# A branch between two expert groups, a deferred embedding, and a last tile in two halves

## The chip, the cores and the metric

The kernel runs on one core of a Trainium2 chip. The metric is the device time of one execution in microseconds (us); lower is better. The core has a matrix engine (PE, with PEld for its weight loads), a vector engine (DVE), a scalar engine (ACT), GpSimd (POOL), and SP, which here only issues transfers. All transfers, from whichever queue, run on the same 16 DMA engines.

## What is computed

One layer: a state-space branch and a convolution branch, an output projection, a layer norm, a mixture of experts, a second layer norm, a gated embedding, and a third layer norm. Only the last three stages bear on the change:

```python
m = hierarchical_moe(h, ...)        # 512 tokens; each goes to 2 of 32 experts
# gate, up = t @ w_gate[e], t @ w_up[e]     (2048 -> 256 each)
# out      = (silu(gate) * up * weight) @ w_down[e]
h = layer_norm(ALPHA * h + m, ln2_g, ln2_b)
e = (p @ w_p) * sigmoid(h @ w_pg + b_pg)    # 2048 -> 2048
x = layer_norm(ALPHA * h + e, ln3_g, ln3_b)
```

Each expert has 6 MB of float32 weights, 192 MB in all, and each is read once.

## The kernel before, in words

**Expert stage.** The 32 experts stand in 14 groups (`GROUPS`), of one, two or four experts each. A group takes up to 128 token rows. The first two groups have two fixed experts each; which experts the others serve is read at run time. A group goes through these steps:

- `gather(i)` (line 1109): POOL fetches the group's token rows into `gx` by an indirect transfer.
- `columns()` (line 1118): PE transposes `gx` in four steps of four blocks; DVE and ACT copy the results to `xt`. There is one `gx` and one `xt`.
- `up` (line 1139), four stages q: each needs one 1 MB load of `w_gu` per expert.
- `act` (line 1146): sigmoid, products, two transposes.
- `down` (line 1159), two stages, each with one 1 MB load of `w_dn` per expert; the result goes to `ob`, and POOL scatters it to `y_dram`.

All weight loads are issued by SP in one order into a ring of 1 MB tiles (`ring_load`, line 1103). A tile is loaded again when PE has read it. The ring has 15 tiles. During group 0 they take that group's 12 loads and the first three of group 1. At the end of group 1 (line 1213) two tiles from the pool `rpool` are put at the front of the ring, so that the next two loads go there. Until then these two tiles hold `w_p`, which the deferred piece of the embedding (lines 1206 to 1212) reads: for the last of the four token tiles, `p @ w_p` is computed after group 1, in 8 products of 512 columns, and written to `p_dram` in two transfers.

**The branch.** If a fixed group has more tokens than its strips hold, an overflow block runs (line 1226). The count is put in `mo` (line 1224), which is the first column of `xt`, so it is written after group 0's first stage has read that column. Every engine reads it into a register and branches by itself. Inputs here take the way around the block. At the end of the way around, SP waits until all the transfers it has issued have landed. The block uses `gx`, `xt` and `ob`. For this reason group 1's gather and columns stand behind it (lines 1279 and 1280), while from group 1 on, the next group's gather stands ahead of `up` and its columns ahead of `down` (lines 1195 and 1200):

```python
if i + 1 < NGR and i:
    gather(sl0[:, i + 1:i + 2])
```

**Order of the work.** The order within each engine's queue is set by a planner with its own model of times; it may move an instruction ahead of the branch if the block doesn't touch what it needs. The program's order gives the priorities.

**Final stage.** For each of four column blocks c of 512 and each token tile m, `f_mm` (line 1330) makes 48 products of 512 columns (16 blocks of the depth, three products each, float32r operands: high and low parts). `gate` (line 1338) adds the bias (DVE), takes the sigmoid (ACT), multiplies by the embedding, adds to `h2` and takes `bn_stats`, all on 512 columns. In the last block, the third layer norm follows for each tile: statistics, a chain of small DVE steps for the inverse root (`rsqrt`), and two passes over two pieces of 1024 columns (`layer_norm`, line 178), each piece then written out (line 1437).

Of the kernel before, what the change touches and what calls it, by code (L numbers as in the profile page):

```python
# [54 lines left out]
def build(tc, I, out, dbg=None, stages=9):  # L55
# [1022 lines left out]
    if True:  # L1078
# [30 lines left out]
        def gather(ig):  # L1109
            G.indirect_dma_start(out=gx, out_offset=None, in_=h_dram,  # L1110
                                 in_offset=bass.IndirectOffsetOnAxis(ap=ig, axis=0), bounds_check=S - 1, oob_is_err=False)
# [75 lines left out]
        early = [loads(0, q) for q in range(6)]  # L1187
        ahead1 = [loads(1, 0)]
        gather(sl1)
        V.tensor_copy(ids_, tab[:, 0:NP])  # L1190
        columns()
        for i, (width, members) in enumerate(GROUPS):
            st = strips(width, members)
            gu = bank("gu", 2)
            if i + 1 < NGR and i:
                gather(sl0[:, i + 1:i + 2])
            for q in range(4):
                up(gu, st, early[q] if i == 0 else ahead1[q] if i == 1 and q < 2 else loads(i, q), q)
            at = act(gu, wt0[:, i:i + 1])
            if i + 1 < NGR and i:  # L1200
                columns()
            for q in range(2):
                down(at, st, early[4 + q] if i == 0 else loads(i, 4 + q), q, sl0[:, NGR + i:NGR + i + 1])
            if i == 1:

                for q in range(2):
                    for c in range(2):
                        ps = bank("dps", 4)
                        for k in range(2):
                            T.matmul(ps, pm[:, k], wps[q][:, k, c * 512:(c + 1) * 512], start=k == 0, stop=k == 1)  # L1210
                        (A.copy if c else V.tensor_copy)(pe_[:, c], ps)
                    G.dma_start(p_dram[NT - 1, 2 * q:2 * q + 2].rearrange("c p d -> p c d"), pe_)
                ring[:0] = [rpool.tile([P, D], FT, name="raw", tag="raw", bufs=2) for _ in range(2)]
            if i == 2:
                for m in range(NT):
                    A.activation(tt[m], tt[m], AF.Identity, scale=ALPHA, bias=zero_of(at[:, 0, 0:1]))
            if i:
                continue
            ahead1.append(loads(1, 1))
            nc.sync.dma_start(pm, I["pT"][:, :, (NT - 1) * P:])  # L1220


            mo = xt[:, 0, 0:1].bitcast(I32)
            V.tensor_copy(mo, tab[:, 2 * NP:])
            most = nc.values_load(mo[0:1], min_val=0, max_val=S)
            with tc.If(most > 0):
                cv, cg = Carve(ob), Carve(gx)
                sv, place = cv.tile([P, 3, 2 * NT]), cv.tile([P, NP])
                pb, v4 = [P, 2 * NT, NP], [P, 2 * NT, 2, NP]
                nc.sync.dma_start(sv.rearrange("p a n -> p (a n)"), sv_dram)  # L1230
                nc.sync.dma_start(place, I["place"][0:1].broadcast_to([P, NP]))
                iot, iof, z = cv.tile([P, P], I32), cv.tile([P, P]), cv.tile([P, 2 * NP])
                tokv, slx = cv.tile([P, 2, NT, 2]), cv.tile([P, NOV, 3 * NP], I32)
                hot = cg.tile([P, 2 * NT, P])
                by_place, vw, val = cv.tile(pb), cv.tile(pb), cg.tile(v4)
                G.iota(iot, pattern=[[1, P]], base=0, channel_multiplier=0)
                V.tensor_copy(iof, iot)
                iop = iot[:, 0:NT]
                G.iota(iop, pattern=[[P, NT]], base=1, channel_multiplier=1)
                for j in range(2):  # L1240
                    V.tensor_copy(tokv[:, j, :, 0], iop)
                    V.tensor_scalar(tokv[:, j, :, 1], tokv[:, j, :, 0], 2.0, float(j - 1), op0=OP.mult, op1=OP.add)
                V.tensor_tensor(by_place, place.unsqueeze(1).broadcast_to(pb), sv[:, 1].unsqueeze(2).broadcast_to(pb), op=OP.is_equal)
                V.tensor_tensor(val, by_place.unsqueeze(2).broadcast_to(v4),
                                tokv.rearrange("p j t a -> p (j t) a").unsqueeze(3).broadcast_to(v4), op=OP.mult)
                V.tensor_tensor(vw, by_place, sv[:, 2].unsqueeze(2).broadcast_to(pb), op=OP.mult)
                for c in range(NOV):
                    slot_hot(hot, iof, sv[:, 0])
                    slot_rows(slx[:, c, 0:2 * NP], hot, z, val.rearrange("p n a e -> p n (a e)"), bank("gu", 2), 2 * NP)
                    slot_weights(slx[:, c, 2 * NP:].bitcast(FT), hot, vw, bank("gu", 2), NP)  # L1250
                    V.tensor_scalar(sv[:, 0], sv[:, 0], -float(P), None, op0=OP.add)
                nc.sync.dma_start(ov_dram, slx)
                V.memset(gx, 0.0)

                with tc.For_i(0, NP, 1) as n:
                    mine = nc.values_load(tab[0:1, bass.ds(n + NP, 1)], min_val=0, max_val=S)
                    with tc.If(mine > 0):
                        e = bass.ds(nc.values_load(tab[0:1, bass.ds(n, 1)], min_val=0, max_val=NE - 1), 1)
                        for c in range(NOV):
                            with tc.If(mine > c * P):  # L1260
                                so = ep.tile([P, 3], I32, name="so")
                                for a in range(3):
                                    nc.sync.dma_start(so[:, a:a + 1], ov_dram[:, c, bass.ds(n + a * NP, 1)])
                                gather(so[:, 0:1])
                                columns()

                                def chunk(q):
                                    nc.sync.dma_start(gx, part(e, q))
                                    return [gx]

                                whole = [(0, slice(0, P))]
                                gu = bank("gu", 2)
                                for q in range(4):
                                    up(gu, whole, chunk(q), q)
                                at = act(gu, so[:, 2:3].bitcast(FT))
                                for q in range(2):
                                    down(at, whole, chunk(4 + q), q, so[:, 1:2])
                                V.memset(gx, 0.0)
            gather(sl0[:, 1:2])
            columns()  # L1280

    s5.close()

# [1 line left out]
    with ExitStack() as s5:  # L1285
# [8 lines left out]
        fpws = [fh.tile([P, 512], FT, name=f"fpw{j}") for j in range(2)]  # L1294
        fsgs = [fh.tile([P, 512], FT, name=f"fsg{j}") for j in range(2)]
        bpgs = [fh.tile([P, 512], FT, name=f"bpg{j}") for j in range(2)]
        st3 = fh.tile([P, NT, 4, 6], FT, name="st3")
        wF = s5.enter_context(tc.tile_pool(reuse_waits="tile", name="wF", bufs=1))
        fystk = ExitStack()
        fy = fystk.enter_context(tc.tile_pool(reuse_waits="tile", name="fy", bufs=1))  # L1300
# [26 lines left out]
        hls.append(wsplit(wF, raws[3], 8, (G, G)))  # L1327
        w_pg = ahead([lambda c=c, q=q: wsplit(wF, raw_load(I["w_pg"][c, q]), 8) for c in range(1, 4) for q in range(4)], 1)

        def f_mm(ps, m, q, hl):  # L1330
            ms = slice(m * P, (m + 1) * P)
            for kk in range(4):
                wh, wl = hl[kk // 2]
                wv = slice(kk % 2 * 512, kk % 2 * 512 + 512)
                k = 4 * q + kk
                mm3(ps, h2h[:, k, ms], h2l[:, k, ms], wh[:, wv], wl[:, wv], k == 0, k == KD - 1)

        def gate(m, c, ps, bpg):
            cs_ = slice(c * 512, (c + 1) * 512)
            flip[0] ^= 1  # L1340
            o, sg = fpws[flip[0]], fsgs[flip[0]]
            nc.sync.dma_start(o, p_dram[m, c])
            V.tensor_tensor(sg, ps, bpg, op=OP.add)
            A.activation(sg, sg, AF.Sigmoid)
            V.tensor_tensor(sg, o, sg, op=OP.mult)
            V.scalar_tensor_tensor(h2[m][:, cs_], h2[m][:, cs_], ALPHA, sg, op0=OP.mult, op1=OP.add)
            V.bn_stats(st3[:, m, c], h2[m][:, cs_])

        def after(x, v):

# [46 lines left out]
        for c in range(4):  # L1397
# [18 lines left out]
            for m in range(NT):  # L1416
                if c == 0:
# [3 lines left out]
                    if m == NT - 1:  # L1421
# [1 line left out]
                        for t in (bpgs[0], bpgs[1], *fpws):  # L1423
                            V.tensor_copy(t[:, 0:1], h2l[:, KD - 1, S - 1:S].bitcast(FT))
                        A.dma_start(bpg, I["b_pg"][:, 0:512].broadcast_to([P, 512]))
                for q in range(4):
                    f_mm(ps[m], m, q, hls[q])
                if c == 0 and m == NT - 1:
                    for j in range(NT):
                        gate(j, c, ps[j], bpg)  # L1430
                if c == 3:
                    gate(m, c, ps[m], bpg)
                    mean, rstd = ln_stats(fh, st3[:, m], "s")
                    for q in range(2):
                        i = slice(q * 1024, (q + 1) * 1024)
                        layer_norm(h2[m][:, i], h2[m][:, i], mean, rstd, g3[:, i], b3[:, i])
                        nc.sync.dma_start(out[m * P:(m + 1) * P, i], h2[m][:, i])
    top.close()
# [64 lines left out]
```

## Time and profile before

| what | us |
|---|---|
| median of 3 runs (1487.8 to 1489.32) | 1488.04 |
| the profiled execution | 1486.21 |
| its span in the trace | 1484.5 |
| PE busy | 1264.4 (85%) |
| DVE busy | 784.1 (53%) |
| POOL busy | 392.9 (26%) |
| ACT busy | 376.4 (25%) |

The profiled execution took 1.71 us more than its span; that part lies around the trace. Busy shares are means over stages with different limits, so they are read by stretch. In the trace, the expert stage reaches from about 667 to 1236 us and the final stage from there to 1484.5 us.

### The profile page before, as it was taken

The numbers are of one execution on the slowest core, as the hardware profiler recorded it, in microseconds if no ns is written. First come the engines' busy times: TensorE is split into PE (matmuls) and PEld (weight loads), VectorE is DVE, ScalarE is ACT, GpSimd is POOL, SyncE is SP. The second block draws the span as 40 slices with busy tenths as digits, with TensorE's granted clock in tenths as the row PEclk, the third lists the DMA queues.
The fourth block names the chain that finished last, engine by engine and source line by source line (L and its number), as shares of the span: only waits on it lengthen the run. The fifth ranks groups of instructions, "written<-read, shape, count | busy, mean of one in ns | idle before, by whom it ended". The sixth has DMA issues, their size and how long they took to land.

```text
span 1484.5 us, 16536 instructions
## 1 busy us (share of the span) xinstructions
PE 1264.4 (85%) x6128; PEld 805.0 (54%) x6129; DVE 784.1 (53%) x1275; ACT 376.4 (25%) x568; POOL 392.9 (26%) x327
## 2 busy tenths in 40 slices
PE   6999999989999999978488998787767774599996
PEld 4877878777777888843132322221111121388884
DVE  7999899789997643681011110010000006975567
ACT  4336555554333421121012100000000003023210
POOL 0368667864944200010010110000000005600000
PEclk9999999998999999989699999999889996699998
DMA  6344544536531362349659999999999995426413
GB/s 233 110 132 119 153 145 137 146 115 217 218 120 59 115 223 85 110 175 375 271 220 424 422 422 421 420 419 420 418 409 418 415 386 190 142 105 215 141 44 120
DMA packets 97448, 349.90 MB, mean 236 GB/s; under 512 B 29939, under 2 KB 43779, under 8 KB 61707
## 3 DMA queue, kind: packets, MB, share of 16 engines
q1 hardware_dynamic: 51152, 303.21, 52.4%
q10 hardware_dynamic: 38832, 21.38, 5.3%
q0 software_dynamic: 7376, 24.19, 4.2%
q8 instruction: 50, 0.82, 0.2%
q14 instruction: 38, 0.30, 0.1%
HBM read 324.36 MB, written 36.38 MB: 243 GB/s over the span
## 4 chain that ended last, share of the span: by engine, by line
DMA 27%; PE 19%; DVE 4%; issue 1%; ACT 0%; POOL 0%; SPq 0%; DVEq 0%; POOLq 0%; ACTq 0%
DMA ring<-w_gu 16%; DMA ring<-w_dn 8%; PE gu L1144 4%; PE fps L102 3%; PE fps L101 3%; PE fps L100 3%; PE dps L1165 2%; DMA raw<-w_gu 2%; DVE tt L180 1%; PE xtp L1124 1%; DMA gx<-h_dram,sl 1%; DVE tt L181 1%; PE h2p L102 0%; PE h2p L101 0%; PE h2p L100 0%
## 5 line engine op out<-in xcount | busy, mean ns | idle before, releaser
L1144 PE MATMUL gu<-ring,xt 128*32 128x512 f32 (+2 forms) x1112 | 241.3, 654 | 57.2 <-DMA ring<-w_gu 57.2
L237 DVE SCALAR_TENSOR_TENSOR cps<-hc,wdw,cps 128x512 f32<-128x512 f32 x232 | 175.0, 754 | 4.8
L1144 PEld LDWEIGHTS gu<-ring,xt 128*32 128x32 f32 (+2 forms) x1112 | 63.4, 130 | 207.1 <-issue 109.4
L100 PE MATMUL zp<-xh,whi 128*128 128x512 f32 x384 | 157.0, 410 | 10.3 <-ACT whi L79 10.1
L79 ACT CAST whi<-raw 128x1024 fp32r<-128x1024 f32 x116 | 119.4, 1047 | 169.3 <-PE zp L102 58.8
L102 PE MATMUL zp<-xh,wlo 128*128 128x512 f32 x384 | 154.2, 402 | 2.7 <-DVE wlo L80 2.7
L101 PE MATMUL zp<-xl,whi 128*128 128x512 f32 x384 | 154.7, 403 | 1.6 <-DVE xl L80 1.6
L80 DVE TENSOR_TENSOR wlo<-raw,whi 128x1024 fp32r<-128x1024 f32 x90 | 125.6, 1405 | 55.2 <-ACT whi L79 54.3
L1151 DVE TENSOR_TENSOR act<-act,gu 128x256 f32<-128x256 f32 x14 | 5.9, 421 | 240.9 <-ACT act L1150 240.9
L1165 PE MATMUL dps<-ring,at 128*32 128x512 f32 (+2 forms) x520 | 121.1, 621 | 10.1 <-ACT at L1156 5.1
L1114 POOL DMA_INDIRECT y_dram<-ob,sl x28 | 27.8, 993 | 340.3 <-ACT ob L1167 340.0
L1129 DVE COPY xt<-xtp 128x512 f32<-128x512 f32 x28 | 19.4, 692 | 143.1 <-PE xtp L1124 135.0
L80 POOL TENSOR_TENSOR wlo<-raw,whi 128x1024 fp32r<-128x1024 f32 x26 | 70.4, 2707 | 85.8 <-ACT whi L79 73.3
L100 PE MATMUL fps<-whi,h2h 128*128 128x512 f32 x224 | 89.5, 400 | 0.7 <-ACT h2h L79 0.7
L102 PE MATMUL fps<-whi,h2l 128*128 128x512 f32 x224 | 89.7, 401 | 0.0
L101 PE MATMUL fps<-wlo,h2h 128*128 128x512 f32 x224 | 88.9, 398 | 0.0
L100 PEld LDWEIGHTS zp<-xh,whi 128*128 128x128 f32 x384 | 73.5, 192 | 26.2 <-ACT whi L79 10.2
L102 PEld LDWEIGHTS zp<-xh,wlo 128*128 128x128 f32 x384 | 73.3, 191 | 20.6 <-DVE wlo L80 3.9
L101 PEld LDWEIGHTS zp<-xl,whi 128*128 128x128 f32 x384 | 73.4, 191 | 17.3 <-DVE xl L80 2.0
L1165 PEld LDWEIGHTS dps<-ring,at 128*32 128x32 f32 (+2 forms) x520 | 35.6, 128 | 80.6 <-issue 57.9
L1167 DVE COPY ob<-dps 128x512 f32<-128x512 f32 x28 | 19.3, 691 | 103.7 <-PE dps L1165 103.7
L1124 PE MATMUL xtp<-ident,gx 128*128 128x128 f32 x224 | 37.2, 290 | 33.2 <-DMA gx<-h_dram,sl 21.0
(460 smaller groups left out, 2273.0 us busy)
## 6 DMA issues: line engine op xcount, KB each, us to landing
ring<-w_gu SPq DMA_DIRECT2D x117, 1024.0 KB, 21.6
ring<-w_dn SPq DMA_DIRECT2D x55, 1024.0 KB, 20.7
raw<-w_in SPq DMA_DIRECT2D x24, 1024.0 KB, 4.9
raw<-w_o SPq DMA_DIRECT2D x16, 1024.0 KB, 4.8
raw<-w_pg SPq DMA_DIRECT2D x14, 1024.0 KB, 5.5
raw<-w_gu SPq DMA_DIRECT2D x11, 1024.0 KB, 21.8
raw<-w_dn SPq DMA_DIRECT2D x9, 1024.0 KB, 22.2
raw<-y_dram SPq DMA_DIRECT2D x12, 512.0 KB, 5.7
```

What stands on the lines that cost most here:

```text
L79: A.copy(hi, src)
L80: eng.tensor_tensor(lo, src, hi.bitcast(FT), op=OP.subtract)
L100: T.matmul(ps, lh, rh, start=start, stop=False)
L101: T.matmul(ps, lh, rl, start=False, stop=False)
L102: T.matmul(ps, ll, rh, start=False, stop=stop)
L237: V.scalar_tensor_tensor(ps if k < 30 else acc, hc[:, k:k + S], wdw[:, ct, k:k + 1], ps, op0=OP.mult, op1=OP.add)
L1114: G.indirect_dma_start(out=y_dram[q], out_offset=bass.IndirectOffsetOnAxis(ap=isc, axis=0), in_=ob[:, q * 1024:(q + 1) * 1024], in_offset= ...
L1124: T.transpose(ps[:, kk * P:(kk + 1) * P], gx[:, k * P:(k + 1) * P], ident)
L1129: V.tensor_copy(o, ps)
L1144: T.matmul(gu[cols], xt[:, k, cols], raws[j][:, kk * 512:(kk + 1) * 512], start=k == 0, stop=k == KD - 1)
L1165: T.matmul(outs[c][cols], at[:, k, cols], raws[j][:, o:o + 512], start=k == 0, stop=k == 1)
L1167: (A.copy if c else V.tensor_copy)(ob[:, q * 1024 + c * 512:q * 1024 + (c + 1) * 512], outs[c])
```

## The change

Three edits:

1. `mo` becomes a tile of its own, written by DVE right after group 0's columns, from an element of `xt` times zero plus the count. Group 1's gather moves ahead of group 0's `up`, and its columns ahead of group 0's `down`. Inside the overflow block they are made again at the end.
2. The deferred embedding moves from behind group 1 to behind group 3, and the two `rpool` tiles join the ring there, at its end.
3. For the last token tile in the last column block, the products are made in two halves of 256 columns, all of the first half before the second; the gate and `bn_stats` run in halves, the statistics take five entries, and the last layer norm's passes and the output go in pieces of 1024, 512 and 512 columns.

```diff
+        mo = ep.tile([P, 1], I32, name="mo")
         V.tensor_copy(ids_, tab[:, 0:NP])
         columns()
+        V.scalar_tensor_tensor(mo, xt[:, 0, 0:1], 0.0, tab[:, 2 * NP:], op0=OP.mult, op1=OP.add)
         for i, (width, members) in enumerate(GROUPS):
-            if i + 1 < NGR and i:
+            if i + 1 < NGR:
                 gather(sl0[:, i + 1:i + 2])
...
-            if i + 1 < NGR and i:
+            if i + 1 < NGR:
                 columns()
...
-            if i == 1:
+            if i == 3:
...
-                ring[:0] = [rpool.tile([P, D], FT, name="raw", tag="raw", bufs=2) for _ in range(2)]
+                ring += [rpool.tile([P, D], FT, name="raw", tag="raw", bufs=2) for _ in range(2)]
...
-            mo = xt[:, 0, 0:1].bitcast(I32)
-            V.tensor_copy(mo, tab[:, 2 * NP:])
             most = nc.values_load(mo[0:1], min_val=0, max_val=S)
             with tc.If(most > 0):
...
-            gather(sl0[:, 1:2])
-            columns()
+                gather(sl0[:, 1:2])
+                columns()
...
-        st3 = fh.tile([P, NT, 4, 6], FT, name="st3")
+        st3 = fh.tile([P, NT, 5, 6], FT, name="st3")
...
-        def f_mm(ps, m, q, hl):
+        def f_mm(ps, m, q, hl, cols=slice(0, 512)):
...
-                wv = slice(kk % 2 * 512, kk % 2 * 512 + 512)
+                wv = slice(kk % 2 * 512 + cols.start, kk % 2 * 512 + cols.stop)
...
+                mm3(ps[:, cols], h2h[:, k, ms], h2l[:, k, ms], wh[:, wv], wl[:, wv], k == 0, k == KD - 1)
+        def gate(m, c, ps, bpg, parts=1):
...
+            for n in range(parts):
+                i = slice(n * 512 // parts, (n + 1) * 512 // parts)
+                h = h2[m][:, c * 512 + i.start:c * 512 + i.stop]
+                V.tensor_tensor(sg[:, i], ps[:, i], bpg[:, i], op=OP.add)
+                A.activation(sg[:, i], sg[:, i], AF.Sigmoid)
+                V.tensor_tensor(sg[:, i], o[:, i], sg[:, i], op=OP.mult)
+                V.scalar_tensor_tensor(h, h, ALPHA, sg[:, i], op0=OP.mult, op1=OP.add)
+                V.bn_stats(st3[:, m, c + n], h)
...
+                end = c == 3 and m == NT - 1
+                for n in range(2 if end else 1):
+                    for q in range(4):
+                        f_mm(ps[m], m, q, hls[q], slice(256 * n, 256 * n + 256) if end else slice(0, 512))
...
+                    gate(m, c, ps[m], bpg, 2 if end else 1)
+                    mean, rstd = ln_stats(fh, st3[:, m, 0:5 if end else 4], "s")
+                    for i in (slice(0, 1024), slice(1024, 1536), slice(1536, 2048)) if end else (slice(0, 1024), slice(1024, 2048)):
```

## Rows read from the trace of the kernel before

**Rows 1.** The page's second part: bandwidth in 40 equal slices of 37.1 us.

```profile
GB/s 233 110 132 119 153 145 137 146 115 217 218 120 59 115 223 85 110 175 375 271 220 424 422 422 421 420 419 420 418 409 418 415 386 190 142 105 215 141 44 120
```

**Rows 2.** Windows: stretch, length, busy us by engine, granted clock, DMA share, GB/s.

```profile
680.00:722.00 42.00, 21.10 (x92) 7.37 (x90) 2.98 (x5) 2.51 (x5) 3.05 (x3) 0.79 1.01 413
722.00:731.00 9.00, 6.17 (x18) 2.68 (x20) 0.69 (x1) 0.58 (x1) 0.00 (x0) 0.50 0.58 242
731.00:762.00 31.00, 29.53 (x126) 11.16 (x123) 4.87 (x8) 4.17 (x8) 4.58 (x5) 0.99 0.23 79
762.00:772.00 10.00, 6.33 (x18) 2.71 (x17) 1.23 (x2) 0.58 (x1) 0.99 (x2) 1.00 0.97 352
772.00:1220.00 448.00, 351.61 (x1772) 109.02 (x1771) 40.05 (x70) 41.12 (x70) 32.13 (x32) 0.95 1.01 418
```

**Rows 3.** The chain that ended last, in order: start us, us, what.

```profile
714.43 9.47 DMA gx<-h_dram,sl
...
873.26 23.72 DMA ring<-w_gu
...
1198.31 21.68 DMA ring<-w_gu
```

**Rows 4.** Line 1226, the branch: operation, count, ns min/median/max, first and last start.

```profile
L1226 SPq EVENT_SEMAPHORE  x9: 17/17/17, 713.0 to 730.6; - x9
...
L1226 PEldq COMPARE_BRANCH  x1: 6519/6519/6519, 699.2 to 699.2; - x1
...
L1226 SPq COMPARE_BRANCH  x1: 50/50/50, 707.6 to 707.6; - x1
```

**Rows 5.** Waits of SP's queue, 700 to 780 us: total, times, longest.

```profile
SPq L1106 <- PE dps L1210: 32.6, 2, 29.8
```

**Rows 6.** Timeline of SP's queue: start us, us, operation, count.

```profile
705.74 1.82 SPq L1106 DMA_DIRECT2D ring<-w_dn  x4
760.59 3.77 SPq L1106 DMA_DIRECT2D raw<-w_gu  x2
```

**Rows 7.** Timeline of PE, groups 0 to 2, same columns, idle before in brackets.

```profile
684.79 7.09 PE L1144 MATMUL gu<-ring,xt 128*64 128x512 f32 x32
...
694.26 8.79 PE L1165 MATMUL dps<-ring,at 128*64 128x512 f32 x32 [0.46 <-ACT at L1156]
724.04 1.09 PE L1124 MATMUL xtp<-ident,gx 128*128 128x128 f32 x4 [21.00 <-DMA gx<-h_dram,sl]
...
737.07 0.66 PE L1124 MATMUL xtp<-ident,gx 128*128 128x128 f32 x4
...
756.86 7.13 PE L1210 MATMUL dps<-raw,pm 128*128 128x512 f32 x16
...
767.72 2.84 PE L1144 MATMUL gu<-raw,xt 128*128 128x512 f32 x6 [3.29 <-DMA raw<-w_gu]
```

**Rows 8.** The page's DMA issues: count, KB each, median us to landing.

```profile
ring<-w_gu SPq DMA_DIRECT2D x117, 1024.0 KB, 21.6
...
raw<-w_in SPq DMA_DIRECT2D x24, 1024.0 KB, 4.9
```

**Rows 9.** Timeline of DVE at the end.

```profile
1467.07 2.48 DVE L181 SCALAR_TENSOR_TENSOR tt<-tt,lny,b 128x1024 f32<-128x1024 f32 x2
1469.72 0.69 DVE L1343 TENSOR_TENSOR fsg<-fps,bpg 128x512 f32<-128x512 f32 x1 [0.17 <-PE fps L102]
...
1472.56 0.69 DVE L1347 BATCH_NORM_STATS2 st<-tt 128x6 f32<-128x512 f32 x1
```

**Rows 10.** Timeline of PE: plain float32 products of 512 columns, then small ones.

```profile
651.05 3.60 PE L846 MATMUL zp<-raw,el 128*128 128x512 f32 x8
654.48 1.86 PE L196 MATMUL cps<-rsc 128*128 128x28 f32 x16
```

**Rows 11.** The chain, near the end: one float32r product of 512 columns.

```profile
1453.82 0.23 PE fps L102
```

**Rows 12.** The page's groups: a DVE operation on 256 columns: busy, mean ns.

```profile
L1151 DVE TENSOR_TENSOR act<-act,gu 128x256 f32<-128x256 f32 x14 | 5.9, 421 | 240.9 <-ACT act L1150 240.9
```

More of the change, by code (lines that the diff above doesn't have):

```diff
@@ L1333, in f_mm @@
                 wh, wl = hl[kk // 2]
-                wv = slice(kk % 2 * 512, kk % 2 * 512 + 512)
+                wv = slice(kk % 2 * 512 + cols.start, kk % 2 * 512 + cols.stop)
                 k = 4 * q + kk
-                mm3(ps, h2h[:, k, ms], h2l[:, k, ms], wh[:, wv], wl[:, wv], k == 0, k == KD - 1)
-        def gate(m, c, ps, bpg):
-            cs_ = slice(c * 512, (c + 1) * 512)
+                mm3(ps[:, cols], h2h[:, k, ms], h2l[:, k, ms], wh[:, wv], wl[:, wv], k == 0, k == KD - 1)
+        def gate(m, c, ps, bpg, parts=1):
             flip[0] ^= 1
@@ L1342, in gate @@
             nc.sync.dma_start(o, p_dram[m, c])
[L1343 to L1347, printed above, removed]
+            for n in range(parts):
[6 more added lines that the diff above has]
+                V.bn_stats(st3[:, m, c + n], h)
         def after(x, v):
@@ L1425, in build @@
                         A.dma_start(bpg, I["b_pg"][:, 0:512].broadcast_to([P, 512]))
-                for q in range(4):
-                    f_mm(ps[m], m, q, hls[q])
+                end = c == 3 and m == NT - 1
+                for n in range(2 if end else 1):
+                    for q in range(4):
+                        f_mm(ps[m], m, q, hls[q], slice(256 * n, 256 * n + 256) if end else slice(0, 512))
                 if c == 0 and m == NT - 1:
@@ L1431, in build @@
                 if c == 3:
[L1432 to L1435, printed above, removed]
+                    gate(m, c, ps[m], bpg, 2 if end else 1)
+                    mean, rstd = ln_stats(fh, st3[:, m, 0:5 if end else 4], "s")
+                    for i in (slice(0, 1024), slice(1024, 1536), slice(1536, 2048)) if end else (slice(0, 1024), slice(1024, 2048)):
                         layer_norm(h2[m][:, i], h2[m][:, i], mean, rstd, g3[:, i], b3[:, i])
```

## Prediction

> **What bounds the kernel now.** I began with the bandwidth by slices. From slice 22 on, for some 450 us, the core moves about 420 GB/s; just before that stand two slices of 271 and 220 [rows 1]. So the expert stage is a stream of weights at a flat top, with a hole near its start. Windows locate it: 413 GB/s from 680 to 722 us, 242 to 731, 79 to 762, 352 to 772, then 418 for 448 us [rows 2]. The chain of waits confirms that the stream sets the end: from 873.26 to 1198.31 us it is 16 links of weight transfers, one handing over to the next [rows 3]. A microsecond of missing flow before that is paid at the end. Taking 418 GB/s as full, the hole costs 9 x (1 - 242/418) + 31 x (1 - 79/418) + 10 x (1 - 352/418) = 3.8 + 25.1 + 1.6 = 30.5 us.
>
> Who made the hole? SP issued group 1's last load just after 707 and the next one at 760.59 [rows 6]. Two things lie between. First the branch: SP branches at 707.6, its semaphore steps end at 730.6 [rows 4]; it waits for its own transfers to land. Then the wait of up to 29.8 us for the embedding's products [rows 5]: group 2's first load goes to a tile that holds `w_p`, and PE reads that only from 756.86 on [rows 7]. PE is that late because it stood idle for 21.00 us before group 1's transposes [rows 7]: their gather, behind the branch, was issued at 714.43 and took 9.47 [rows 3].
>
> **Edit 1, gather and columns of group 1 ahead.** The gather can go when group 0's transposes have read `gx`, about 684.8 (PE's next products start at 684.79 [rows 7]). At 9.47 us it lands near 694.3, just where `down` of group 0 starts (694.26 [rows 7]). On POOL only group 0's scatter stands behind it, and that isn't ready yet. Columns cost PE 4 x 0.66 = 2.6 us at full clock [rows 7], so `down` ends near 705.7 instead of 703.05. `up` of group 1 can start at about 706 to 708, since PE passes the branch at 699.2 + 6.5 = 705.7 now [rows 4]. It takes 2 x 7.09 = 14.2 us; then 2.4 from `up` to `down` (684.79 + 7.09 to 694.26), and 8.8 for `down`: PE is through with group 1 near 733, not 756.9. The later end of `down(0)` frees ring tiles up to 2.6 us later; the stream has a backlog then (413 GB/s until 722 [rows 2]), so I take nothing, bound 0 to 2.6. The new `mo` is one DVE step on one column in place of another, and SP's branch stands behind group 1's loads as now [rows 4, 6]: nothing. The copies inside the block aren't run.
>
> **Edit 2, embedding behind group 3, `rpool` tiles at the ring's end.** Group 2's loads now go to tiles that group 0 and group 1's first products have freed by about 714. SP can issue when it is past the branch, 730.6 instead of 760.59. What remains of the hole: the fall of flow while SP's last loads land, 3.8 us as now, and the restart. A 1 MB load into a quiet queue lands in 4.9 [rows 8], of which 1.05 MB / 418 GB/s = 2.5 is flow, so 2.4 are lost. Gain: 30.5 - 3.8 - 2.4 = 24.3 us.
>
> A second way to the same number: group 2 starts on PE at 767.72 [rows 7]; now about 730.6 + 4.9 + 1 for two gathers in between = 736.5, so 31.2 earlier. But what flowed in the hole (79 GB/s x 31 us = 2.4 MB of gathers and scatters [rows 2]) must flow in the full stream, 5.9 us. That leaves 25.3. I take 24.3.
>
> Two costs are counted at nothing. The embedding's 7.13 us of PE [rows 7] move from a stretch in which PE waited anyway to one in which loads are ahead of PE; the stream hides them, since PE waits for it from 873 on [rows 3]. Without that cover: +7.1. And the ring has 15 tiles instead of 17 until group 5. Some nine loads are under way (21.6 us to landing [rows 8] at 2.5 each), so about six tiles hold loads that wait for PE. Groups 2 to 4 have 24 loads and take PE about 3 x 28 us (14.2 + 2.4 + 8.8 + 2.6 by the terms above), in which the stream could bring 31: seven ahead, close to the limit. I take 0, bound +3.
>
> **Edit 3, the last tile.** Products: 48 of 0.227 us (start to start; 0.23 rounded [rows 11]) = 10.9 become 96 of 256 columns. The trace has no float32r product of 256. Nearest rows: 16 small products with full weight loads take 1.86, 0.116 each [rows 10], so weight loads repeat at that step; half of 0.227 is 0.114. I take 0.12: 96 x 0.12 = 11.5, +0.6. From above: plain float32 products take 0.45 per instruction and two instructions per 512 columns (3.60 for 8 [rows 10]), so 0.45 for 256 columns; that end is a rival below.
>
> Gate: from the add (1469.72) to the end of `bn_stats` (1473.25) pass 3.5 us [rows 9]. On 256 columns a DVE step takes 0.42 instead of 0.69 [rows 12], so the second half alone takes about 2.3. But DVE isn't free: the layer norm of the tile before ends at 1469.55 [rows 9], in step with PE, so the first half's four steps (4 x 0.45 = 1.8) delay the second unless they find gaps. With DVE free at 1471.4, `bn_stats` ends at 1473.7, +0.5; in the best case (all hidden), -1.2 + 0.6 = -0.6; in the worst, no overlap, +1.1. The two passes get one instruction more each, +0.1 in all. The last piece out is half as big: 0.52 MB to 0.26 MB, -0.6 at 418 GB/s. Sum: +0.5 + 0.1 - 0.6 = 0.0, bounds -1.1 to +1.2.
>
> In the trace, the gate's add starts 0.17 us after the tile's last product [rows 9], and no row shows DVE reading a bank that PE is still filling. The Trainium skill speaks against this edit here (PSUM — Partial Sum Buffer, Terms): a matrix write and a DVE or ACT access to one bank at the same time is an error, reads included. Both halves lie in one bank, so by that rule the first half's gate has to wait for the second half's products, and edit 3 would come to the worst case, about +0.6 with the output's gain. By the overlap it would be 0.0. No run here shows which; the sum does not depend on it.
>
> **Sum.** 24.3 + 0.0, so 1486.21 - 24.3 = 1461.9 against the profiled execution. That execution lies 1.8 us below the median of the runs, 1488.04; I expect the same distance, so 1464.
>
> **Rivals.**
> - *The hole closes altogether.* The planner may put group 2's first three loads, whose tiles group 0 frees, ahead of SP's branch, and scatter and gather may fill the wait behind it. For it: SP issued all nine of group 1's late loads before its branch [rows 6]. Against it: whatever is issued before, SP still waits for it to land. Price: the whole 30.5, so 1457.5.
> - *PE is held at the branch as SP is.* If `up` of group 1 needs something that is settled only when SP is through (730.6), PE ends group 1 near 730.6 + 14.2 + 2.4 + 8.8 = 756, 11.7 ahead of 767.72, while the loads are 24.3 ahead and stop at a full ring. The gain lies between the two; half way 18, so 1470. For it: the block touches `xt`. Against it: PE's own branch ended at 705.7 [rows 4].
> - *It doesn't do what it says.* The planner keeps some load of group 2 behind the embedding or behind group 1's products; the hole stays, little changes: 1486.
> - *Slower: the half products run at the plain float32 rate.* Place: the last tile on PE, with nothing behind it to hide in. Price: 96 x 0.45 = 43.2 against 10.9, +32.3, so 1464 + 32.3 = 1496. It decides once a half product takes more than (10.9 + 24.3) / 96 = 0.37 us. Against it: the full ones run four times faster than plain ones, and 256 columns are still over twice the weight load's 128.
>
> **Chances.** Forecast 0.60, with 1460 to 1468 as its own range; the hole closed 0.17; PE held 0.15; no effect 0.05; slower products 0.03. The range 1455 to 1475 takes in the first two and most of the third, with the bounds of edits 1 to 3 (-1.1 to +6.8). About 0.2%, 3 us, is what a measurement here can tell from no change. The first three cases are faster, 0.92, with half of the fourth 0.94; the other half is no change, 0.03; slower 0.03.
>
> **What would show it.** In the changed kernel's trace: group 1's gather on POOL near 685, its transposes before `down(0)` and no 21 us idle before them; SP's next weight load after the branch near 731 and no wait for line 1210's products among its longest; bandwidth back at 418 by about 737; the chain all weight transfers from there, the last at about 1196 instead of 1220; the embedding's products behind group 3 without PE starving later. Last tile: 96 products about 0.12 apart, the span's end 15 us after the last, as now. I am wrong if SP still stands at the branch much beyond 731, if flow breaks again between 760 and 870 (a full ring), or if the final stage, from the last scatter to the end, changes by more than 2 us.

## Result, and the profile after

| | before | after |
|---|---|---|
| median of the runs (us) | 1488.04 | 1461.51 (3 runs, 1460.5 to 1463.85) |
| profiled execution (us) | 1486.21 | 1461.51 |
| its span (us) | 1484.5 | 1459.8 |

The ratio of the runs is 0.9822, 95% interval 0.9800 to 0.9845: faster, as forecast, and 2.5 us below the 1464 that was forecast. Between the profiled executions the gain is 24.7 us; the sum had 24.3.

The span's 24.7 us can be followed on the chain of waits. The last weight transfer before the end of the stream ends at 1197.25 us (before: 1198.31 + 21.68 = 1219.99 [rows 3]), 22.7 earlier. From there to the final stage's first product on `h2p` it is 77.7 us instead of 79.3, and from that product to the end 184.8 instead of 185.2. So 22.7 come from the stream, 1.6 less than the sum had, and 2.0 from the final stage, where the sum had nothing.

First the bandwidth in 40 slices, now of 36.5 us. The two slices of 271 and 220 [rows 1] have become 408 and 368.

```profile
GB/s 236 114 132 122 155 119 153 152 115 168 258 122 89 90 225 116 67 165 304 408 368 422 423 423 418 419 416 418 417 406 414 418 353 183 149 125 198 149 52 107
```

The windows of the changed kernel (columns as in [rows 2]) show what is left of the hole: 9 x (1 - 361/418) + 14 x (1 - 301/418) = 1.2 + 3.9 = 5.1 us, where 30.5 stood.

```profile
680.00:722.00 42.00, 31.29 (x135) 11.79 (x136) 4.36 (x7) 3.68 (x7) 4.06 (x4) 0.88 1.01 410
722.00:731.00 9.00, 8.67 (x42) 3.07 (x38) 0.44 (x2) 0.38 (x1) 0.00 (x0) 1.00 0.87 361
731.00:745.00 14.00, 7.08 (x20) 3.64 (x21) 1.35 (x3) 0.96 (x2) 0.00 (x0) 0.76 0.76 301
745.00:762.00 17.00, 17.00 (x57) 6.38 (x56) 1.70 (x3) 1.76 (x3) 3.02 (x3) 1.00 1.01 420
...
772.00:1196.00 424.00, 337.66 (x1753) 103.74 (x1751) 39.97 (x65) 35.94 (x67) 33.63 (x34) 0.94 1.01 417
```

SP's timeline in the changed kernel answers to [rows 6]: its first load after the branch now goes out at 733.66 us, not 760.59, and it is a `ring` load, no longer one into a tile that the embedding reads.

```profile
706.01 3.05 SPq L1106 DMA_DIRECT2D ring<-w_dn  x4
733.66 2.56 SPq L1106 DMA_DIRECT2D ring<-w_gu  x4
```

At the branch itself hardly anything has changed for SP (line 1226, columns as in [rows 4]). It branches at 709.1, its first step after that comes 5.5 us later, and its last at 733.4. PE's branch instruction takes 6052 ns.

```profile
L1226 SPq EVENT_SEMAPHORE  x9: 17/17/17, 714.6 to 733.4; - x9
...
L1226 PEldq COMPARE_BRANCH  x1: 6052/6052/6052, 707.8 to 707.8; - x1
...
L1226 SPq COMPARE_BRANCH  x1: 50/50/50, 709.1 to 709.1; - x1
```

PE's timeline answers to [rows 7]. The wait of 21.00 us is gone. Group 1's four transposes stand behind `down` of group 0 (from 702.90 on); then PE waits 6.47 us for its own queue at the branch, and 6.28 us for the first load of group 2, whose first stage the planner has put ahead of `down` of group 1 (747.95).

```profile
694.16 8.81 PE L1165 MATMUL dps<-ring,at 128*64 128x512 f32 x32 [0.46 <-ACT at L1156]
702.90 0.66 PE L1124 MATMUL xtp<-ident,gx 128*128 128x128 f32 x4
...
714.30 15.79 PE L1144 MATMUL gu<-ring,xt 128*64 128x512 f32 x64 [6.47 <-PEq L1226]
...
738.58 5.35 PE L1144 MATMUL gu<-ring,xt 128*128 128x512 f32 x8 [6.28 <-DMA ring<-w_gu]
...
747.95 4.50 PE L1165 MATMUL dps<-ring,at 128*64 128x512 f32 x18
```

The chain of waits runs over PE (the embedding included) until 892.46 and over weight transfers alone from there to 1197.25.

```profile
801.53 7.06 PE dps L1212 x16
...
892.46 24.39 DMA ring<-w_dn
...
1175.91 21.34 DMA ring<-w_gu
```

Last, DVE at the end, which answers to [rows 9]. Both halves' adds stand in one row, after the tile's last product; add to end of `bn_stats` is 1447.73 - 1444.73 = 3.0 us, not 3.5.

```profile
1441.46 2.48 DVE L181 SCALAR_TENSOR_TENSOR tt<-tt,lny,b 128x1024 f32<-128x1024 f32 x2
1444.73 0.76 DVE L1345 TENSOR_TENSOR fsg<-fps,bpg 128x256 f32<-128x256 f32 x2 [0.79 <-PE fps L102]
...
1446.98 0.75 DVE L1349 BATCH_NORM_STATS2 st<-tt 128x6 f32<-128x256 f32 x2
```

### The profile page after: what moved, and what is told of

Same layout as the page of the kernel before. It is cut to its first block, busy times and chain, and to the rows that moved or that the text cites. A ratio compares the mean times of both kernels' runs of the same rounds, so it can differ in the third digit from the quotient of the medians.

```text
span 1459.8 us, 16654 instructions
## 1 busy us (share of the span) xinstructions
PE 1262.2 (86%) x6176; PEld 807.9 (55%) x6177; DVE 785.2 (54%) x1281; ACT 377.1 (26%) x569; POOL 391.3 (27%) x327
## 5 line engine op out<-in xcount | busy, mean ns | idle before, releaser
L1144 PE MATMUL gu<-ring,xt 128*32 128x512 f32 (+2 forms) x1128 | 250.4, 647 | 57.4 <-DMA ring<-w_gu 51.0
L1144 PEld LDWEIGHTS gu<-ring,xt 128*32 128x32 f32 (+2 forms) x1128 | 68.4, 131 | 201.0 <-issue 107.1
L1165 PE MATMUL dps<-ring,at 128*32 128x512 f32 (+2 forms) x536 | 124.3, 624 | 12.5 <-DMA ring<-w_dn 7.4
L100 PE MATMUL fps<-whi,h2h 128*128 128x512 f32 (+1 forms) x240 | 91.7, 383 | 0.7 <-ACT h2h L79 0.7
L102 PE MATMUL fps<-whi,h2l 128*128 128x512 f32 (+1 forms) x240 | 92.1, 384 | 0.0
L101 PE MATMUL fps<-wlo,h2h 128*128 128x512 f32 (+1 forms) x240 | 91.2, 381 | 0.0
L1110 POOL DMA_INDIRECT gx<-h_dram,sl x14 | 14.5, 1037 | 165.6 <-PE xtp L1124 152.5
## 6 DMA issues: line engine op xcount, KB each, us to landing
ring<-w_dn SPq DMA_DIRECT2D x57, 1024.0 KB, 21.2
raw<-w_gu SPq DMA_DIRECT2D x9, 1024.0 KB, 22.6
```

Source lines behind the costliest of these rows:

```text
L100: T.matmul(ps, lh, rh, start=start, stop=False)
L101: T.matmul(ps, lh, rl, start=False, stop=False)
L102: T.matmul(ps, ll, rh, start=False, stop=stop)
L1144: T.matmul(gu[cols], xt[:, k, cols], raws[j][:, kk * 512:(kk + 1) * 512], start=k == 0, stop=k == KD - 1)
L1165: T.matmul(outs[c][cols], at[:, k, cols], raws[j][:, o:o + 512], start=k == 0, stop=k == 1)
```

## Experiments

The theory was: the stream's hole is the whole cost; SP made it, by waiting for tiles that the embedding reads; the rest of the change is worth nothing. The main rival: PE's lateness (21 us idle, then the embedding) is the cost. All ratios below are against the kernel before, on the same chip, with 95% intervals.

### One edit at a time

**edit1**: the kernel before with edit 1 alone (`mo`, gather and columns moved).

> The kernel before with edit 1 alone: group 1's gather and columns ahead, the embedding still behind group 1, the two pool tiles still at the ring's front. Theory (the stream's hole is what pays): group 2's first load still waits for the embedding's products. PE is through the branch near 714, group 1's up ends near 730, down near 741, the embedding's first products near 745; the first load of group 2 goes out near 745 instead of 760.6, so about 15 us are gained: 1473. Rival (PE's idle time of 21 us was the cost, whoever waits for it): the whole 24, so 1464.

Measured: 1472.77 us, ratio 0.9902 (0.9872 to 0.9931). The theory's number. In the profiled execution PE is through with group 1 and the embedding 17.5 us earlier (the embedding begins at 739.32, not 756.86), so SP gets the pool tiles that much earlier, at 743.05. (Some 2.0 us of this are an earlier start: group 0's last `up` begins at 682.78, not 684.79.) The windows still hold 9 x (1 - 272/418) + 14 x (1 - 110/418) + 17 x (1 - 379/418) = 15.0 us of hole:

```profile
722.00:731.00 9.00, 7.54 (x42) 3.25 (x40) 1.59 (x4) 1.24 (x3) 0.00 (x0) 1.00 0.65 272
731.00:745.00 14.00, 14.00 (x50) 5.19 (x46) 2.59 (x4) 2.34 (x4) 3.81 (x4) 1.00 0.33 110
745.00:762.00 17.00, 12.44 (x30) 5.66 (x29) 1.38 (x2) 0.86 (x2) 0.76 (x1) 0.80 0.98 379
```

**edit2**: the kernel before with edit 2 alone.

```diff
-            if i == 1:
+            if i == 3:
...
-                ring[:0] = [rpool.tile(...) for _ in range(2)]
+                ring += [rpool.tile(...) for _ in range(2)]
```

> The kernel before with edit 2 alone: the embedding behind group 3 and the two pool tiles at the ring's end; group 1's gather and columns stay behind the branch. Theory (the stream's hole): SP issues group 2's first loads when it is past the branch, near 731, three at once into free tiles and the others as PE reads group 1's from 727 on; PE ends group 1 near 757, so the ring is full at times; gain between 15 and 24, so 1468. Rival (PE's idle time decides): the 21 us of idle time stay, and only the embedding's 7.1 us leave the path: 1481.

Measured: 1463.04 us, ratio 0.9839 (0.9810 to 0.9869). Better than my own theory had it, and the rival is out: edit 2 alone brings nearly everything, although PE still stands idle for 21.40 us before group 1. SP's first load of group 2 goes out at 729.64, and the last weight transfer ends at 1195.36.

```profile
724.79 1.08 PE L1124 MATMUL xtp<-ident,gx 128*128 128x128 f32 x4 [21.40 <-DMA gx<-h_dram,sl]
```

PE catches up later: the chain goes over to the transfers at 925.05 instead of 892.46, and has two more short pieces of PE from 971.96 on. SP waits for ring tiles much more (70.0 us in 38 waits for `up`'s products, 12.0 in 18 in the changed kernel), but the flow from 772 to 1196 is 417 GB/s in both. In this run SP's waits for tiles, with other transfers under way, did not break the stream.

**no_tail** and **tail_only**: edit 3 taken back in the changed kernel, and edit 3 alone in the kernel before.

> The changed kernel with edit 3 undone: the last tile has whole products of 512 columns, one gate and two output pieces again. Theory (the expert stage's stream made the whole gain, the last tile about nothing): in the changed kernel's trace the stretch from the add of the tile before to the end is 26.6 us against 25.7 in the kernel before, so undoing edit 3 gives 1461.5 - 0.9 = 1460.6, and the gap of bandwidth near 731 us stays as in the changed kernel. Rival (edit 3 made part of the gain, through the final stage, which is 2.6 us shorter from the first read of the experts' results to the end): 1464 or more, and that stretch is back at 246 us.

> The kernel before with edit 3 alone. Theory: about nothing, by the changed kernel's own trace +0.9, so 1488 to 1489; 96 products at 0.120 us start to start; both halves of the gate's add only after the last product. Rival (the halves overlap with the gate and gain): 1486.5 or less, with the first half's add before the last product's end.

Measured: no_tail 1462.75 us, ratio 0.9820 (0.9793 to 0.9847), beside 0.9822 for the full change; tail_only 1487.87, ratio 1.0001 (0.9984 to 1.0017). Edit 3 moves nothing that can be measured, from either side. By its median no_tail lies between the two forecasts (1460.6 and 1464), so the ratios decide; its windows hold 9 x (1 - 389/418) + 14 x (1 - 285/418) = 5.1 us of hole, as in the changed kernel. In tail_only both adds again stand behind the last product, and its tail, from the second last tile's add to the end of the span, is 26.25 us against 25.66 before.

### Which half of edit 2

**ring_only** is the kernel before with one line changed; **edit1_ringend** adds edit 1 to it. In both the embedding stays behind group 1.

```diff
-                ring[:0] = [rpool.tile(...) for _ in range(2)]
+                ring += [rpool.tile(...) for _ in range(2)]
```

> The kernel before with edit 1, and the two pool tiles at the ring's end instead of its front; the embedding stays behind group 1. It tells which half of edit 2 matters. Theory (what held SP was that group 2's first load went to a tile that the embedding reads; PE's time for the embedding is covered wherever it stands): 1460 to 1464, SP's first load of group 2 near 730 to 734. Rival (the embedding's place on PE decides, 7 us ahead of group 2): 1468 to 1473, SP's first load near 743, as with edit 1 alone.

> The kernel before with one line changed: the two pool tiles join the ring at its end instead of its front; gather, columns, embedding and last tile stay. Theory (the hole came from SP's wait for two tiles that the embedding still reads; PE being late by 21 us costs little as long as the ring does not run out): SP's first load of group 2 near 730 instead of 760.59, 1462 to 1466. Rival (PE, 21 us late by the gather and 7 us more by the embedding, starts group 2 as late as before, near 767, and the ring fills): 1470 to 1480.

Measured: edit1_ringend 1464.50 us, ratio 0.9861 (0.9843 to 0.9880), SP's first load at 732.61; ring_only 1465.67, ratio 0.9858 (0.9835 to 0.9881), first load at 731.87. SP's first load goes out when the theory said in both; the times lie near the upper end of its ranges (edit1_ringend half a microsecond above) and clear of the rivals. The one line makes 1.42 of the 1.78% of the whole change, with PE late by its 21 us and the embedding ahead of group 2. The loads into the pool tiles now come 28.5 us after the first one (timeline of SP's queue in ring_only), when the embedding (756.64 to 763.77) is freeing them; SP still waits for its products, but 2.7 us at the longest where it was 29.8 [rows 5]:

```profile
731.87 2.56 SPq L1106 DMA_DIRECT2D ring<-w_gu  x4
...
760.37 3.77 SPq L1106 DMA_DIRECT2D raw<-w_dn  x2
```

PE's idle time in ring_only, and its windows:

```profile
725.23 1.09 PE L1124 MATMUL xtp<-ident,gx 128*128 128x128 f32 x4 [21.54 <-DMA gx<-h_dram,sl]
```

```profile
722.00:731.00 9.00, 4.99 (x16) 2.44 (x18) 0.69 (x1) 0.58 (x1) 0.00 (x0) 0.50 0.71 296
731.00:745.00 14.00, 14.00 (x64) 4.63 (x62) 0.69 (x1) 0.58 (x1) 1.00 (x1) 0.95 0.87 343
```

Its hole is 9 x (1 - 296/418) + 14 x (1 - 343/418) = 5.1 us, the changed kernel's. In the profiled executions the last weight transfer ends at 1197.61 us in ring_only, 1195.86 in edit1_ringend and 1197.25 in the changed kernel: in the stream the one line is worth as much as all three edits. By the medians the embedding's new place and edit 1 add 3 to 4 us on top of the line, by the ratios 5 to 6; the intervals just overlap that of the whole change. In the traces such a gain would lie behind the stream (264.6 and 263.3 us from its end to the end of the span, against 262.6), not in it; whether it is one stays open.

### What hides the embedding

**embed_x4**: the changed kernel with the deferred embedding's products made four times.

```diff
-                        for k in range(2):
-                            T.matmul(ps, pm[:, k], wps[q][:, k, c * 512:(c + 1) * 512], start=k == 0, stop=k == 1)
+                        for k in range(8):
+                            T.matmul(ps, pm[:, k % 2], wps[q][:, k % 2, c * 512:(c + 1) * 512], start=k % 2 == 0, stop=k % 2 == 1)
```

> The changed kernel with the deferred embedding's products behind group 3 made four times over (same values): 32 products in place of 8, 3 x 7.06 = 21.2 us more of PE. Theory (the stream hides the embedding there, PE's lateness is free as long as the ring does not fill): 1461.5 to 1464.5, the weight stream at 415 GB/s or more through 800 to 900, and the chain's PE part reaching beyond 892. Rival (PE bounds groups 2 to 6, since the chain runs over PE until 892): most of the 21 is paid, 1475 to 1483, with a dip in flow behind 800.

Measured: 1470.49 us, ratio 0.9879 (0.9862 to 0.9895). Both numbers miss: about 9 of the 21 us are paid. The profiled execution was long (1480.22) and reached the expert stage some 6.5 us late, so only what happens inside the stage is read from it. There it isn't PE's work as such that costs: SP comes to the first of the two pool tiles at 818.6 us, `w_p` is read in it until 825 and in the second until 839, and SP stands still with every load behind it. SP's waits from 800 to 850 us, then its timeline:

```profile
SPq L1106 <- PE dps L1212: 20.2, 2, 13.6
```

```profile
825.19 14.51 SPq L1106 DMA_DIRECT2D raw<-w_dn  x2
```

Two slices of that run drop to 357 and 340 GB/s. It is the mechanism of the kernel before, made again behind group 3. In the changed kernel the same two loads go out with a wait of 0.3 us at most: the first at 813.96, the second at 816.7, 8.1 us after the embedding's end (801.53 + 7.06 = 808.6). That is the slack that the forecast's "nothing" rests on; 21.2 us more of PE less 8.1 of slack is 13.1, near the longest wait of 13.6.

```profile
813.96 3.10 SPq L1106 DMA_DIRECT2D raw<-w_dn  x2
```

### What is left of the hole

**no_branch**: the changed kernel without the overflow block and the read of its count. **branch_end**: both moved behind the last group.

> The changed kernel without its overflow block and without the read of the count: it leaves out the handling of overflowing tokens, which these inputs don't need. Theory (what is left of the hole, 9 x (1 - 361/418) + 14 x (1 - 301/418) = 5.1 us, is SP waiting at the branch for its own transfers and restarting): the windows from 722 to 745 show 415 GB/s or more, PE has no idle 6.5 us before up of group 1, and the time is 1461.5 - 5.1 = 1456.4. Rival (the planner's order and the scatter and gather traffic make the dip, not the branch): flow still falls to 300 to 360 GB/s there and the time is 1460 or more.

> The changed kernel with the read of the count, the branch and the overflow block moved behind the last expert group. Theory: SP no longer drains in the middle of the stream, so the 5.1 us of hole go; behind the last group SP has little under way, so the drain costs only the branch itself, some 5.4 us between SP's branch and its next instruction, partly beside the last scatter: 1457 to 1461.5. Rival (the branch is paid in full at the end, where nothing covers it, and it stops the final stage's loads from being issued ahead): 1464 to 1475.

Measured: no_branch 1460.25 us, ratio 0.9823 (0.9808 to 0.9838); branch_end 1462.30, ratio 0.9832 (0.9815 to 0.9849). The rest of the hole is the branch's: without it the windows are flat, and PE starts `up` of group 1 at 703.29, with no wait for its queue.

```profile
722.00:731.00 9.00, 7.09 (x26) 2.11 (x24) 0.90 (x2) 0.76 (x2) 0.00 (x0) 0.85 1.01 421
731.00:745.00 14.00, 13.21 (x52) 6.35 (x49) 2.77 (x4) 1.76 (x3) 1.98 (x2) 1.00 1.01 419
```

But the time hardly follows. In no_branch the last weight transfer ends 3.7 us earlier (1193.58), the span only 1.9 (1457.9), because the final stage takes 1.8 us longer from there; the medians differ by 1.3, inside the intervals. The theory was right on the hole and wrong on the 5.1 us. Where the final stage loses its 1.8 stays open; from the stream's end to the end of the span it takes 264.3 us here, 264.5 in the kernel before, 263.3 to 264.9 in the profiled executions of the runs above, and 262.6 in the changed kernel, so it is the changed kernel's that is short. In branch_end the flow is as flat (421 and 419 GB/s), and the price comes back at the end: POOL passes the branch only after issuing the last scatter (1210.5) and is through with its semaphore steps at 1217.2; the final stage's first load of `y` goes out at 1217.69 instead of 1215.63. On the chain:

```profile
1210.44 0.35 SPq L1310
1210.79 6.39 another core or an unknown queue
1217.69 0.57 SPq L1321
```

Neither place of the branch is measurably better, and what its absence is worth lies within the noise (1.3 us by the medians, nothing by the ratios).

### The last tile by itself

**two_banks**: the second half's products go to another bank of PSUM. **whole_products**: products on 512 columns, gate in halves and three output pieces kept.

```diff
+                ps_b = bank("h2p", 2) if end else None
...
-                        f_mm(ps[m], m, q, hls[q], slice(256 * n, 256 * n + 256) if end else slice(0, 512))
+                        f_mm(ps[m] if n == 0 else ps_b, m, q, hls[q], slice(256 * n, 256 * n + 256) if end else slice(0, 512))
...
-                V.tensor_tensor(sg[:, i], ps[:, i], bpg[:, i], op=OP.add)
+                V.tensor_tensor(sg[:, i], (ps_b if n else ps)[:, i], bpg[:, i], op=OP.add)
```

> The changed kernel with the two halves of the last tile's products in two banks of PSUM. Theory (the bank that both halves share makes the first half's gate wait for the last product): the first half's add starts some 5.7 us before the last product's end, and from the last add to the end of bn_stats it takes some 2.3 us instead of 3.0; in the total some -0.7, too small to be seen in the time. Rival (DVE is busy with the tile before, or the order on DVE holds the add): the first half's add still comes after the last product, 3.0 us.

> The changed kernel with the last tile's products on 512 columns again; the gate in halves and the output in three pieces stay. Theory: the last tile's products take 10.9 us instead of 11.5 and the gate stays at 3.0, so the stretch from the second last tile's add to the end of the span falls from 26.6 to 26.0. Rival (the halves of the products feed the halves of the gate): the gate grows back to 3.5 and the stretch stays at 26.5.

One profiled execution each (1463.53 and 1463.26 us), read by their last rows; all times from the second last tile's add.

| us | before | no_tail | whole_products | after | two_banks |
|---|---|---|---|---|---|
| to the last tile's (last) add | 10.88 | 10.88 | 10.88 | 11.51 | 11.51 |
| that add to end of `bn_stats` | 3.53 | 3.53 | 3.01 | 3.00 | 4.52 |
| second last tile's add to end of span | 25.66 | 25.98 | 25.94 | 26.58 | 28.03 |

whole_products comes out as the theory said: the half products cost 0.63, the gate in halves gains 0.5 by itself, for while ACT works on one half DVE works on the other. two_banks comes out worse than either expectation. The first half's add does start early, 5.8 us before the second's (1439.52 and 1445.28 on DVE's timeline), as the theory said, but DVE waits 2.22 us for it with the layer norm of the tile before queued behind; that layer norm then stands in front of the second half's last steps.

```profile
1439.52 0.42 DVE L1345 TENSOR_TENSOR fsg<-fps,bpg 128x256 f32<-128x256 f32 x1 [2.22 <-PE fps L102]
...
1446.53 2.48 DVE L181 SCALAR_TENSOR_TENSOR tt<-tt,lny,b 128x1024 f32<-128x1024 f32 x2
1448.92 0.42 DVE L1348 SCALAR_TENSOR_TENSOR tt<-tt,fsg 128x256 f32<-128x256 f32 x1
```

## Why the prediction was right, step by step

- **The hole is what counts, and SP makes it.** Right, and shown by edit1, edit2, ring_only, edit1_ringend and embed_x4. The size is less exact. By the windows the changed kernel should gain 30.5 - 5.1 = 25.4 us, and the stream's end came 22.7 earlier; about 1.3 of the difference is a flow of 410 and 417 GB/s where it had been 413 and 418, the rest stays open. In edit1 the windows give 30.5 - 15.0 = 15.5, and the stream's end came 17.4 earlier, of which 2.0 are that execution's earlier start. So the mechanism holds, but that the whole gain of 24.7 came out at the forecast's 24.3 is in part luck: the stream gave 1.6 less, and the final stage 2.0 that were in no term.
- **What remains: 6.2 us forecast, 5.1 measured.** SP left the branch at 733.4, not 730.6, but transfers flowed longer behind it. That the remainder is the branch's is shown by no_branch.
- **"PE is that late because it stood idle", edit 1.** The gather went out on POOL at 685.04, as forecast. But the planner put the columns behind `down` of group 0, not ahead; so PE met the branch with nothing to do and lost 6.47 us to it, a wait that the kernel before hid behind `down` and that the forecast didn't list. `up` of group 1 started at 714.30, not at 706 to 708; group 2 at 738.58, not 736.5. None of it shows in the time. What the prediction didn't see is that edit 1 itself is worth next to nothing once the ring's order is changed: it has 1.0% alone and nothing measurable beside the one line (0.9861 against 0.9858).
- **Embedding behind group 3 at nothing.** Right, but for another reason than given. The forecast looked at PE, which waits for the stream from 873 on, and expected only weight transfers on the chain from 737; the chain ran over PE, the embedding included, until 892.46, and still the flow stood at 417 GB/s. embed_x4 shows what the cover is: the 8.1 us between the last product on `w_p` and the load into its tile.
- **15 tiles instead of 17 at nothing.** Right: flow of 416 GB/s or more from slice 22 to 29, with SP's waits for tiles at most 5.3 us long. The forecast was nearer to a full ring than it said: 84 us at 2.5 are 33 loads, not 31.
- **Edit 3 at 0.0, bounds -1.1 to +1.2.** Measured +0.92 in the tail: +0.63 for the products, as forecast, and -0.53 for the gate, together +0.1 where the sum had +0.5 for both; +0.26 for the two passes (+0.1); and +0.5 behind the last pass, for the output (-0.6). Apart from the products the terms were mis-sized. The output's +0.5 is uncertain itself: from the last pass to the end of the span it is 4.1 us in the kernel before and 4.4 in no_tail, which have two pieces, and 4.3 in tail_only and 4.6 in the changed kernel, which have three. The forecast gain of 0.6 isn't there in any case. For it I had divided bytes by the full flow. In the last stretch the median from issue to landing is 2.7 us for pieces of 512 KB and 3.1 for those of 256 KB, so a smaller last piece lands no sooner.
- **The shared bank.** Both adds stand behind the last product, so the overlap that the sum assumed didn't happen. The Trainium skill (PSUM — Partial Sum Buffer, Terms) calls it an error when PE writes a bank while DVE reads it. The trace agrees in that no add runs beside the products in the shared bank; the tail grew by 0.92, and by 0.59 in tail_only, where that rule was put at +0.6. With a second bank the first add starts 5.8 us ahead of the second (two_banks); since the second half then also has a tile of its own, no run here tells the bank from the tile.
- **The final stage.** I had named a change of more than 2 us there, from the last scatter to the end, as a sign of being wrong. It lies right at that mark: from the last scatter's landing it is 244.5 us instead of 246.5 (2.0 less), from the first read of `y` 2.6 less. In the kernel before, DVE has three splits of the next weights to do in front of the first rows of `y` (chain of waits, below): the rows landed at 1242.55 and DVE took them up at 1247.16. In the changed kernel they landed at 1222.64 and were taken up at 1222.91. The 4.3 us saved there are in part lost again, because the rows landed 25.4 us behind the stream's end instead of 22.6. This was luck of the order, not part of the sum: in edit2 and no_tail the splits again stand in front of the first rows.

```profile
1238.33 4.22 DMA y<-y_dram
...
1242.61 2.40 DVE wlo L80 x2
...
1245.95 1.21 DVE wlo L80
1247.16 1.67 DVE tt L1370
```

- **The forecast's 1464 against 1461.51.** Of the 2.5 us, 1.8 is the distance between profiled execution and median, which I carried over and which was zero this time; 0.4 is what the two misses above leave of each other (-1.6 and +2.0), the rest rounding.
- **Rivals.** The hole didn't close altogether. PE was held at the branch, by 6.5 us, but not until SP was through. No effect, and products at the plain float32 rate, are out: the half products are 11.51 / 96 = 0.120 us apart. (256 columns are twice the weight load's 128, not over twice.)

## What to carry to other kernels

When one queue issues all loads in order, the tile that a load goes to matters more than who reads it: a load into a tile that is still read stops every load behind it. Put tiles that come free late at the end of the ring, not at its front; here one line did most of a three-part change, and a slow engine's 21 us of idle time cost little once it no longer held the loads. And take an overlap that an order of instructions promises only after asking what is queued behind the waiting instruction: with two banks the earlier start made the tail longer.

## What the runs showed of the hardware

- A taken branch took very different times on different engines. SP's next step came 5.1 to 5.6 us after it in the stream, and PE's branch instruction took 6.03 to 6.52 us there and 3.43 at the end of the stream (branch_end); DVE, ACT and POOL, at the same branch, took their next step 0.5 to 0.6 us after it. The Trainium skill (Runtime: NRT & Kernel Launch, Instruction fetch mechanics) says that a jump to a place beyond the instructions already fetched has to wait for a transfer of them; the rows agree with that in kind, but that page has no time for it. In the kernel before, the changed kernel, edit1, edit2 and branch_end the DMA view shows one 0.02 MB transfer on an instruction queue inside PE's branch; no run here tells this cause from others.
- A float32r product of 256 columns takes 0.120 us from start to start where one of 512 takes 0.227: 6% more for the same columns.
- Two operations of DVE on 256 columns in a row take 0.75 to 0.76 us together, one on 512 takes 0.69.
